# Per-layer input moved into the last MLP product, and the final norm's root without activation tables

## The chip, the cores and the metric

The kernel runs on one core of a Trainium2 chip. The metric is the device time of one execution in microseconds (us). Engines are named as in the profile: PE is TensorE's matmul and PEld its weight load, DVE is VectorE, ACT is ScalarE, POOL is GpSimd, SP is SyncE, which issues nearly all DMAs.

## The reference

A hybrid decoder layer on 512 tokens of width 1024, all in float32. Only its end is touched:

```python
u = rmsnorm(x, norm_mlp_g[i]) @ w_up[i]
x = x + jnp.square(jax.nn.relu(u)) @ w_down[i]

gate = jax.nn.sigmoid(rmsnorm(x, norm_ple_g[i]) @ w_ple_gate[i])
x = x + gate * (p[i].astype(x.dtype) @ w_ple_proj[i])
return rmsnorm(x, final_norm_g)
```

Ahead of it stand a mixer (a chunkwise mLSTM and sliding-window attention on one normalised input) and its output projection. `rmsnorm(x, g)` is `x * rsqrt(mean(x * x) + 1e-6) * g`, taken per token.

## The kernel before

**Exact products from two halves.** A float32 operand is split in two float32r tiles: the high part is a cast on ScalarE (line 134), the low part the rest, a subtraction on VectorE (line 135). A product is then three matmuls, high by high, high by low and low by high (`pairs`, line 154). Every weight is loaded whole by a DMA from SyncE into one of four buffers `wr` (`load_raw`, line 141) and split into one of four pairs `wh`, `wl` (`load_w`, line 146). Where a gain or scale is to be applied on the way, the split is lines 137 and 138.

**The order of the work.** The program is written in plain order, and Tile, the layer under it, sets the order of instructions on each engine by its own estimate of when inputs are ready, with earlier lines going first among what is ready. Each engine then runs its list in order, waiting on semaphores. SyncE's queue of DMAs is such a list too. A tile pool is a piece of SBUF; when a pool is closed, a later pool may lie on the same bytes, and a tile there waits for the readers of the tile that lay there.

**The MLP.** The 4096 hidden columns are done in four quarters (line 920). `up(q)` makes eight blocks of `uf`: matmul, relu with the token's scale, square, four sums in tile F (lines 856 to 859), split (line 861; the two halves of `uf`). `down(q)` (line 864) is a Strassen-Winograd product with seven block products instead of eight: weights are loaded into `wd` and `wr`, summed on VectorE (lines 886, 890, 904 and 910), split and multiplied, and `acc` (line 881) adds each finished PSUM pair to the residual XK (line 883). There are three such pairs of PSUM banks, X, Y and Z; line 896 adds to the running block p1. Pool `mp` holds F, rB and rt, pool `np_` holds p1, the `uf` halves and `wd`.

**The tail, lines 926 to 1003.** Both pools are closed and pool `tp` opened. The final gain is loaded to all partitions (`gfin`, line 932). For each of four token blocks of 128, p is loaded (`ptok`, line 935), transposed on TensorE (line 938) and split into `pT` (line 940). `ple(nh)` (line 942) multiplies it by one half of its projection, 24 matmuls of 512 columns, and ScalarE copies the result to `pe` (line 947). `columns_of` (line 784) makes x2, the transposed residual with its gain: for each of eight columns of 128, four transposes (line 788) into one bank of a PSUM pair and a split (lines 137 and 138). Lines 957 to 961 take the squares of each token (line 960) and the reciprocal root of their mean, `rk`: ScalarE's Sqrt (line 250) and VectorE's reciprocal (line 252).

Then the gate. Its first 512 columns are summed over four chunks of weights for all four token blocks (lines 990 to 993, 96 matmuls of 512 columns), the second 512 per token block in two halves of 256 columns from two PSUM buffers (lines 997 to 1002, 192 matmuls of 256 columns). `gate` (line 966) evicts: sigmoid with scale rk (line 968), product with `pe` (973), sum into the residual (975), sum of squares (976), and a product with `gfin` on GpSimd (977). `final(m)` (line 979) adds three sums of squares (981 and 982), takes the reciprocal root (250 and 252), scales two halves (985) and stores each (986). Line 971 is a dummy Sqrt that has the table loaded behind the last sigmoid. Sigmoid and Sqrt are in different tables of ScalarE; Square and Copy run with either.

Of the kernel before, what the change touches and what calls it, by code (L numbers as in the profile page):

```python
# [10 lines left out]
F32 = mybir.dt.float32  # L11
F32R = mybir.dt.float32r
AF = mybir.ActivationFunctionType
ALU = mybir.AluOpType
AX = mybir.AxisListType

P = 128
# [19 lines left out]
def block_kernel(  # L37
# [33 lines left out]
    def pool(stack, name, **kw):  # L71
        return stack.enter_context(tc.tile_pool(name=name, bufs=1, reuse_waits="tile", **kw))
# [13 lines left out]
    def nm(s):  # L86
        n_names[0] += 1
        return f"{s}_{n_names[0]}"


    def ps_g():
        return pp.tile([P, 512], F32, tag="g", bufs=2, name=nm("psg"))
# [38 lines left out]
    def split(dst, src, scale=None):  # L131

        if scale is None:
            A.copy(dst[0], src)  # L134
            V.tensor_sub(dst[1], src, r32(dst[0]))  # L135
        else:
            A.activation(dst[0], src, AF.Copy, scale=scale)
            V.scalar_tensor_tensor(dst[1], src, scale, r32(dst[0]), ALU.mult, ALU.subtract)
# [645 lines left out]
    def columns_of(dst, k, g):  # L784

        ps = pair()[:, 0, :]
        for m in range(NT):
            T.transpose(ps[:, m * P : (m + 1) * P], xk[m][:, k * P : (k + 1) * P], ident)
        split(dst[k], ps, g[:, k : k + 1])
# [22 lines left out]

    st_a.close()
    st_m, st_n = ExitStack(), ExitStack()
    mp = pool(st_m, "mp")
    np_ = pool(st_n, "np")
    F = lambda: mp.tile([P, 8, 256], F32, tag="F", bufs=1, name=nm("F"))

    A21, A11, A22, A12, S1, S2, S3, S4 = range(8)
# [44 lines left out]
    def down(q, uf):  # L864
# [52 lines left out]
            prod(Z, S4, form(b22[kh]), kh, False, True)  # L917
        acc(Z, 1, 1)

    for q in range(4):  # L920
        uf = []
        up(q, uf)
        down(q, uf)


    st_n.close()
    st_m.close()
    tp = pool(ctx, "tp")
    pT = [[tp.tile([P, 512], F32R, name=nm("pT")) for _ in range(2)] for _ in range(2)]
    pe = [tp.tile([P, D], F32, name=nm("pe")) for _ in range(NT)]  # L930
    gfin = tp.tile([P, D], F32, name="gfin")
    nc.sync.dma_start(out=gfin, in_=g_fin.broadcast_to([P, D]))
    for m in range(NT):
        t = tp.tile([P, PLE], F32, tag="ptok", bufs=4, name=nm("ptok"))
        nc.sync.dma_start(out=t, in_=p[m * P : (m + 1) * P, :])
        ps = ps_g()
        for k in range(2):
            T.transpose(ps[:, k * P : (k + 1) * P], t[:, k * P : (k + 1) * P], ident)
        for k in range(2):
            split([q[:, m * P : (m + 1) * P] for q in pT[k]], ps[:, k * P : (k + 1) * P])  # L940

    def ple(nh):
        w = load_w(w_pp[nh], 2 * 512, 2)
        for m in range(NT):
            ps = ps_g()
            mm_tok(ps, w, pT, m)
            A.copy(pe[m][:, nh * 512 : (nh + 1) * 512], ps)

    ple(0)
    ple(1)  # L950
    x2b, x2 = big_hl("x2")
    for k in range(8):
        columns_of(x2, k, gple)
    rk = []
    warm = cp.tile([P, 1], F32, name="warm")
    fs = cp.tile([P, NT, 4], F32, name="fs")
    for m in range(NT):
        junk = tp.tile([P, D], F32, tag="junk", bufs=1, name=nm("junk"))
        ss = small("ss", 1)
        A.activation(junk, xk[m], AF.Square, accum_out=ss)  # L960
        rk.append(rstd_of(ss, D))

    def tmp(n):
        return tp.tile([P, 512], F32, tag="tmp", bufs=8, name=nm(n))
# [1 line left out]
    def gate(m, c, n, ps):  # L966
        sg = tmp("sgp")
        A.activation(sg[:, :n], ps, AF.Sigmoid, scale=rk[m])
        if m == NT - 1 and c == D - 256:

            A.activation(warm, sg[:, :1], AF.Sqrt, bias=eps_t, scale=0.0)
        pr = tmp("prod")[:, :n]
        V.tensor_mul(pr, sg[:, :n], pe[m][:, c : c + n])
        part = xk[m][:, c : c + n]
        V.tensor_add(part, part, pr)
        A.activation(sg[:, :n], part, AF.Square, accum_out=fs[:, m, c // 256 : c // 256 + 1])
        G.tensor_tensor(part, part, gfin[:, c : c + n], ALU.mult)

    def final(m):
        ss = small("fss", 1)  # L980
        V.tensor_add(ss, fs[:, m, :1], fs[:, m, 2:3])
        V.tensor_add(ss, ss, fs[:, m, 3:])
        rs = rstd_of(ss, D)
        for c in (slice(0, 512), slice(512, D)):
            V.tensor_scalar_mul(xk[m][:, c], xk[m][:, c], rs)
            nc.sync.dma_start(out=out[m * P : (m + 1) * P, c], in_=xk[m][:, c])

    a, b = pair(), pair()
    pv = [a[:, 0, :], a[:, 1, :], b[:, 0, :], b[:, 1, :]]
    for c in range(4):  # L990
        w = load_w(w_pg[c], 2 * 512, 2)
        for m in range(NT):
            mm_tok(pv[m], w, x2[2 * c : 2 * c + 2], m, first=c == 0, last=c == 3)
    for m in range(NT):
        gate(m, 0, 512, pv[m])
    wg = [load_w(w_pg[4 + c], 2 * 512, 2) for c in range(4)]
    for m in range(NT):
        for o in (0, 256):
            ps = ps_g()[:, :256]
            for c in range(4):  # L1000
                mm_tok(ps, [q[:, :, o : o + 256] for q in wg[c]], x2[2 * c : 2 * c + 2], m, first=c == 0, last=c == 3)
            gate(m, 512 + o, 256, ps)
        final(m)

# [91 lines left out]
```

## Time and profile before

| | |
|---|---|
| three runs | 955.58, 956.19, 957.11 us, median 956.19 |
| the profiled execution | 955.62 us, span 953.9 us |
| mean granted clock of TensorE | 0.989 |
| busy: PE, DVE, ACT, POOL | 909.8, 645.6, 461.4, 33.4 us |
| chain that ended last, by engine | PE 83%, DVE 7%, ACT 5%, DMA 2%, issue 2% |

The profile is one execution. A group of instructions is named by line, engine, operation and tiles (out<-in), with its count and shape; `| busy, mean ns | idle before <-releaser` gives its busy time in us, the mean time of one in ns, and how long its engine stood idle just ahead of it and what ended that. A line is often that of a helper, so tiles tell where in the program one is: `x<-psp,gple` is x2's split, `wl<-wr` a weight's low half. In a timeline a row is start, length, engine, line, operation, tiles and count (instructions of one kind in a row are merged). A matmul's recorded length holds its drain through the array, so several in a row take less each than one alone.

### The profile page before, as it was taken

The numbers are of one execution on the slowest core, as the hardware profiler recorded it, in microseconds if no ns is written. First come the engines' busy times: TensorE is split into PE (matmuls) and PEld (weight loads), VectorE is DVE, ScalarE is ACT, GpSimd is POOL, SyncE is SP. The second block draws the span as 40 slices with busy tenths as digits, with TensorE's granted clock in tenths as the row PEclk, the third lists the DMA queues.
The fourth block names the chain that finished last, engine by engine and source line by source line (L and its number), as shares of the span: only waits on it lengthen the run. The fifth ranks groups of instructions, "written<-read, shape, count | busy, mean of one in ns | idle before, by whom it ended". The sixth has DMA issues, their size and how long they took to land.

```text
span 953.9 us, 11756 instructions
## 1 busy us (share of the span) xinstructions
PE 909.8 (95%) x4498; PEld 743.4 (78%) x4498; DVE 645.6 (68%) x992; ACT 461.4 (48%) x772; POOL 33.4 (3%) x49
## 2 busy tenths in 40 slices
PE   7959999989999999999999999999999999989995
PEld 5748999867877667788888887888788788867785
DVE  6877877454887874455654578757967885797365
ACT  7543544343685675544222545334434533435546
POOL 1000000000000000000210000000000000000032
PEclk9979999998999999999999999999999999999999
DMA  7221333631111131243352520631252063104202
GB/s 277 79 89 45 133 142 128 217 114 64 45 67 45 66 111 66 67 133 111 133 198 89 199 89 1 199 117 37 89 185 79 1 197 112 45 1 155 67 1 88
DMA packets 28602, 97.31 MB, mean 102 GB/s; under 512 B 3969, under 2 KB 4481, under 8 KB 28546
## 3 DMA queue, kind: packets, MB, share of 16 engines
q1 hardware_dynamic: 27074, 91.32, 27.9%
q0 software_dynamic: 1472, 5.24, 1.6%
q8 instruction: 35, 0.57, 0.2%
q14 instruction: 21, 0.17, 0.1%
HBM read 89.21 MB, written 7.34 MB: 101 GB/s over the span
## 4 chain that ended last, share of the span: by engine, by line
PE 83%; DVE 7%; ACT 5%; DMA 2%; issue 2%; SPq 0%; DVEq 0%; ACTq 0%
PE psg L162 49%; PE psp L162 20%; PE psa L162 6%; DVE wl L135 2%; PE pst L700 2%; ACT wh L134 2%; PE pst L627 1%; PE pst L162 1%; PE pst L690 1%; DVE uf L135 1%; PE psa L619 1%; ACT lm L601 1%; PE psa L582 1%; DMA xt<-in_x 1%; PE psa L583 1%
## 5 line engine op out<-in xcount | busy, mean ns | idle before, releaser
L135 DVE TENSOR_TENSOR wl<-wr,wh 128x1024 fp32r<-128x1024 f32 (+1 forms) x136 | 174.7, 1287 | 109.6 <-ACT wh L134 105.0
L134 ACT CAST wh<-wr 128x1024 fp32r<-128x1024 f32 (+1 forms) x136 | 142.5, 1050 | 218.5 <-PE psg L162 106.6
L162 PE MATMUL psg<-x,wh 128*128 128x512 f32 x512 | 160.1, 393 | 0.0
L162 PE MATMUL psp<-wh,uf 128*128 128x512 f32 x448 | 141.1, 394 | 2.0 <-DVE uf L135 2.0
L162 PE MATMUL psg<-h,wh 128*128 128x512 f32 x384 | 124.3, 403 | 0.6 <-DVE qs L547 0.6
L162 PEld LDWEIGHTS psg<-x,wh 128*128 128x128 f32 x512 | 96.1, 188 | 21.2
L162 PEld LDWEIGHTS psp<-wh,uf 128*128 128x128 f32 x448 | 83.8, 188 | 23.3 <-DVE uf L135 3.7
L162 PE MATMUL psg<-x,wl 128*128 128x512 f32 x256 | 100.5, 393 | 0.0
L162 PE MATMUL psp<-wl,uf 128*128 128x512 f32 x224 | 88.0, 393 | 2.0 <-DVE wl L135 2.0
L162 PEld LDWEIGHTS psg<-h,wh 128*128 128x128 f32 x384 | 71.6, 191 | 20.9 <-issue 6.6
L134 ACT CAST wh<-wd 128x1024 fp32r<-128x1024 f32 x44 | 45.9, 1051 | 70.5 <-PE psp L162 34.0
L162 PE MATMUL psg<-h,wl 128*128 128x512 f32 x192 | 76.5, 398 | 0.0
L135 DVE TENSOR_TENSOR wl<-wd,wh 128x1024 fp32r<-128x1024 f32 x44 | 53.0, 1220 | 8.8 <-ACT wh L134 8.5
L162 PEld LDWEIGHTS psg<-x,wl 128*128 128x128 f32 x256 | 48.1, 188 | 10.7
L162 PEld LDWEIGHTS psp<-wl,uf 128*128 128x128 f32 x224 | 42.1, 188 | 11.9 <-DVE wl L135 2.4
L135 DVE TENSOR_TENSOR uf<-F,uf 128x1792 fp32r<-128x1792 f32 x16 | 32.4, 2023 | 21.8 <-ACT uf L134 21.8
L162 PEld LDWEIGHTS psg<-h,wl 128*128 128x128 f32 x192 | 36.6, 191 | 9.5 <-issue 1.6
L162 PE MATMUL psg<-yb,wh 128*128 128x512 f32 x128 | 42.5, 408 | 0.0
L850 DVE SCALAR_TENSOR_TENSOR rt<-psg,rB 128x512 f32<-128x512 f32 x32 | 22.0, 688 | 27.8 <-PE psg L162 27.8
L162 PE MATMUL psg<-ya,wh 128*128 128x512 f32 x128 | 39.9, 393 | 0.0
L134 ACT CAST uf<-F 128x1792 fp32r<-128x1792 f32 x16 | 27.1, 1695 | 24.7 <-DVE F L859 24.7
L162 PE MATMUL psa<-h,wh 128*128 128x256 f32 x192 | 35.1, 284 | 0.2 <-ACT p L449 0.2
(267 smaller groups left out, 1684.3 us busy)
## 6 DMA issues: line engine op xcount, KB each, us to landing
wr<-in_w_up SPq DMA_DIRECT2D x32, 512.0 KB, 4.2
wd<-in_w_down SPq DMA_DIRECT2D x24, 512.0 KB, 4.4
gd<-gr POOLq DMA_DIRECT2D x8, 512.0 KB, 3.0
wr<-in_w_o SPq DMA_DIRECT2D x8, 512.0 KB, 3.3
wr<-in_w_qsw SPq DMA_DIRECT2D x8, 512.0 KB, 4.3
wr<-in_w_qkml SPq DMA_DIRECT2D x8, 512.0 KB, 3.2
wr<-in_w_b SPq DMA_DIRECT2D x8, 512.0 KB, 3.2
gl<-gd SPq DMA_DIRECT2D x8, 512.0 KB, 3.3
```

Source lines behind the costliest of these rows:

```text
L134: A.copy(dst[0], src)
L135: V.tensor_sub(dst[1], src, r32(dst[0]))
L162: last_mm[0] = T.matmul(ps, l, r, start=first and i == 0, stop=last and i == len(ops) - 1, skip_group_check=parts)
L582: T.matmul(o, q[:, n * P : (n + 1) * P], kk[kp][ab][:, k0 : k0 + 256], start=True, stop=False)
L583: T.matmul(o, q[:, n * P : (n + 1) * P], kl[kp][ab][:, k0 : k0 + 256], start=False, stop=True)
L601: A.activation(lm3[:, g, :], lm3[:, g, :], AF.Exp, bias=nmx[:, g : g + 1], accum_out=sm[:, g : g + 1])
L619: T.transpose(pt[:, c : c + P], lm3[ab][:, g, j * P : (j + 1) * P], ident)
L627: T.matmul(o[HALF[ab], :], vs[n + 1 - nk + j][:, c : c + 64], pTs[j][:, ab * 512 : (ab + 1) * 512], start=j == 0, stop=j == nk - 1,)
L690: T.matmul(psc[:, n0:], qk[4 + h][:, n0 : n0 + P], qk[h][:, n0:], start=True, stop=True)
L700: T.matmul(pn[:, : DV + 1], wT[s][:, t * P : (t + 1) * P], vm[s][:, h, :], start=s == 0, stop=s == t)
L850: V.scalar_tensor_tensor(a, ps, 0.0, rB, ALU.max, ALU.mult)
```

## The change

It does four things. p is loaded, transposed and split between `up(3)` and `down(3)` of the MLP, in a pool that lies where `mp` lay (`np_` and `mp` are swapped so that `mp` can be closed first). The first half of p's projection is put between x2's fourth and fifth column, the second half after the eighth, and the squares for `rk` are queued on ScalarE behind the last copy of the projections. The last norm's reciprocal root is taken on VectorE: a first guess from the bits of the sum, then three Newton steps, y <- y (3 - s y^2) / 2 without its signs and halves, which are made good by a factor in `gfin` (-sqrt(1024) / 8192, applied once on VectorE). GpSimd's product with `gfin` is gone: for the first 512 columns VectorE makes the product `z` early and ScalarE scales it, for the last 512 one VectorE instruction does both; the epsilon and two of the three sums are added ahead (`s`). The dummy Sqrt goes.

```diff
 
     st_a.close()
     st_m, st_n = ExitStack(), ExitStack()
+    np_ = pool(st_n, "np")
     mp = pool(st_m, "mp")
-    np_ = pool(st_n, "np")
     F = lambda: mp.tile([P, 8, 256], F32, tag="F", bufs=1, name=nm("F"))
 
     A21, A11, A22, A12, S1, S2, S3, S4 = range(8)
...
             prod(Z, S4, form(b22[kh]), kh, False, True)
         acc(Z, 1, 1)
 
+    def ple_rows():
+
+        ep = pool(st_n, "ep")
+        pT = [[ep.tile([P, 512], F32R, name=nm("pT")) for _ in range(2)] for _ in range(2)]
+        for m in range(NT):
+            t = ep.tile([P, PLE], F32, tag="ptok", bufs=4, name=nm("ptok"))
+            nc.sync.dma_start(out=t, in_=p[m * P : (m + 1) * P, :])
+            ps = ps_g()
+            for k in range(2):
+                T.transpose(ps[:, k * P : (k + 1) * P], t[:, k * P : (k + 1) * P], ident)
+            for k in range(2):
+                split([q[:, m * P : (m + 1) * P] for q in pT[k]], ps[:, k * P : (k + 1) * P])
+        return pT
+
     for q in range(4):
         uf = []
         up(q, uf)
+        if q == 3:
+            st_m.close()
+            pT = ple_rows()
         down(q, uf)
 
 
+    wp0 = load_w(w_pp[0], 2 * 512, 2)
     st_n.close()
-    st_m.close()
     tp = pool(ctx, "tp")
-    pT = [[tp.tile([P, 512], F32R, name=nm("pT")) for _ in range(2)] for _ in range(2)]
     pe = [tp.tile([P, D], F32, name=nm("pe")) for _ in range(NT)]
     gfin = tp.tile([P, D], F32, name="gfin")
     nc.sync.dma_start(out=gfin, in_=g_fin.broadcast_to([P, D]))
-    for m in range(NT):
-        t = tp.tile([P, PLE], F32, tag="ptok", bufs=4, name=nm("ptok"))
-        nc.sync.dma_start(out=t, in_=p[m * P : (m + 1) * P, :])
-        ps = ps_g()
-        for k in range(2):
-            T.transpose(ps[:, k * P : (k + 1) * P], t[:, k * P : (k + 1) * P], ident)
-        for k in range(2):
-            split([q[:, m * P : (m + 1) * P] for q in pT[k]], ps[:, k * P : (k + 1) * P])
-
-    def ple(nh):
-        w = load_w(w_pp[nh], 2 * 512, 2)
+
+    V.tensor_scalar_mul(gfin, gfin, -(D**0.5) / 8192)
+
+    def ple(nh, w):
         for m in range(NT):
             ps = ps_g()
             mm_tok(ps, w, pT, m)
-            A.copy(pe[m][:, nh * 512 : (nh + 1) * 512], ps)
-
-    ple(0)
-    ple(1)
+            evicted = A.copy(pe[m][:, nh * 512 : (nh + 1) * 512], ps)
+        return evicted.ins
+
     x2b, x2 = big_hl("x2")
-    for k in range(8):
+    for k in range(4):
         columns_of(x2, k, gple)
+    ple(0, wp0)
+    for k in range(4, 8):
+        columns_of(x2, k, gple)
+    evicted = ple(1, load_w(w_pp[1], 2 * 512, 2))
     rk = []
-    warm = cp.tile([P, 1], F32, name="warm")
     fs = cp.tile([P, NT, 4], F32, name="fs")
-    for m in range(NT):
-        junk = tp.tile([P, D], F32, tag="junk", bufs=1, name=nm("junk"))
-        ss = small("ss", 1)
-        A.activation(junk, xk[m], AF.Square, accum_out=ss)
-        rk.append(rstd_of(ss, D))
+    with tc.issue_after(evicted):
+        for m in range(NT):
+            junk = tp.tile([P, D], F32, tag="junk", bufs=1, name=nm("junk"))
+            ss = small("ss", 1)
+            A.activation(junk, xk[m], AF.Square, accum_out=ss)
+            rk.append(rstd_of(ss, D))
 
     def tmp(n):
         return tp.tile([P, 512], F32, tag="tmp", bufs=8, name=nm(n))
...
     def gate(m, c, n, ps):
         sg = tmp("sgp")
         A.activation(sg[:, :n], ps, AF.Sigmoid, scale=rk[m])
-        if m == NT - 1 and c == D - 256:
-
-            A.activation(warm, sg[:, :1], AF.Sqrt, bias=eps_t, scale=0.0)
         pr = tmp("prod")[:, :n]
         V.tensor_mul(pr, sg[:, :n], pe[m][:, c : c + n])
         part = xk[m][:, c : c + n]
         V.tensor_add(part, part, pr)
         A.activation(sg[:, :n], part, AF.Square, accum_out=fs[:, m, c // 256 : c // 256 + 1])
-        G.tensor_tensor(part, part, gfin[:, c : c + n], ALU.mult)
-
-    def final(m):
-        ss = small("fss", 1)
-        V.tensor_add(ss, fs[:, m, :1], fs[:, m, 2:3])
-        V.tensor_add(ss, ss, fs[:, m, 3:])
-        rs = rstd_of(ss, D)
-        for c in (slice(0, 512), slice(512, D)):
-            V.tensor_scalar_mul(xk[m][:, c], xk[m][:, c], rs)
-            nc.sync.dma_start(out=out[m * P : (m + 1) * P, c], in_=xk[m][:, c])
+
+    def one(n):
+        return tp.tile([P, 1], F32, tag=n, bufs=4, name=nm(n))
+
+    def inv_sqrt(ss):
+
+
+        bits, y, t = one("bits"), one("iy"), one("it")
+        I = mybir.dt.int32
+        V.tensor_scalar(bits.bitcast(I), ss.bitcast(I), 1, None, ALU.logical_shift_right)
+        V.tensor_scalar(y.bitcast(I), bits.bitcast(I), -1.0, float(0x5F3759DF), ALU.mult, ALU.add)
+        for three in (3.0, 12.0, 768.0):
+            V.tensor_scalar(t, y, y, ss, ALU.mult, ALU.mult)
+            V.tensor_scalar(y, t, three, y, ALU.subtract, ALU.mult)
+        return y
+
+    def final(m, s):
+
+        ss = one("fss")
+        V.tensor_add(ss, fs[:, m, 3:], s)
+        rs = inv_sqrt(ss)
+        A.activation(zs[m], zs[m], AF.Copy, scale=rs)
+        nc.sync.dma_start(out=out[m * P : (m + 1) * P, :512], in_=zs[m])
+        o = xk[m][:, 512:]
+        V.scalar_tensor_tensor(o, o, rs, gfin[:, 512:], ALU.mult, ALU.mult)
+        nc.sync.dma_start(out=out[m * P : (m + 1) * P, 512:], in_=o)
 
     a, b = pair(), pair()
     pv = [a[:, 0, :], a[:, 1, :], b[:, 0, :], b[:, 1, :]]
...
         w = load_w(w_pg[c], 2 * 512, 2)
         for m in range(NT):
             mm_tok(pv[m], w, x2[2 * c : 2 * c + 2], m, first=c == 0, last=c == 3)
+    zs = []
     for m in range(NT):
         gate(m, 0, 512, pv[m])
+        zs.append(tp.tile([P, 512], F32, name=nm("z")))
+        V.tensor_mul(zs[m], xk[m][:, :512], gfin[:, :512])
     wg = [load_w(w_pg[4 + c], 2 * 512, 2) for c in range(4)]
     for m in range(NT):
         for o in (0, 256):
...
             for c in range(4):
                 mm_tok(ps, [q[:, :, o : o + 256] for q in wg[c]], x2[2 * c : 2 * c + 2], m, first=c == 0, last=c == 3)
             gate(m, 512 + o, 256, ps)
-        final(m)
+            if o == 0:
+                s = one("fse")
+                V.tensor_scalar(s, fs[:, m, :1], fs[:, m, 2:3], D * EPS, ALU.add, ALU.add)
+        final(m, s)
```

## The prediction

> **What bounds the kernel now.** I read the page's busy times first, then busy times by stretch over the last 112 us, then TensorE's own waits there, then the timelines of the engines it waited for. A stretch's row holds its length, busy time and instructions of PE, PEld, DVE, ACT and POOL, then TensorE's granted clock, DMA share and GB/s; a wait's row holds us in total, times and the longest.
>
> ```profile
> PE 909.8 (95%) x4498; PEld 743.4 (78%) x4498; DVE 645.6 (68%) x992; ACT 461.4 (48%) x772; POOL 33.4 (3%) x49
> ```
> ```profile
> 842.00:854.00 12.00, 9.70 (x41) 7.37 (x41) 11.77 (x12) 3.15 (x3) 0.00 (x0) 1.00 0.01 2
> 854.00:875.75 21.75, 21.75 (x94) 17.69 (x95) 16.35 (x14) 8.30 (x8) 0.00 (x0) 1.00 0.28 96
> 875.75:887.87 12.12, 9.24 (x56) 6.80 (x54) 9.00 (x21) 11.40 (x29) 0.00 (x0) 1.00 0.41 132
> 887.87:898.90 11.03, 11.03 (x50) 9.01 (x48) 2.45 (x2) 5.65 (x9) 0.00 (x0) 1.00 0.28 94
> 898.90:917.82 18.92, 18.92 (x84) 15.39 (x82) 6.78 (x8) 7.23 (x8) 0.00 (x0) 1.00 0.09 29
> 917.82:934.07 16.25, 12.14 (x98) 11.52 (x96) 11.70 (x17) 9.90 (x22) 8.60 (x6) 1.00 0.02 5
> 934.07:945.74 11.67, 11.66 (x96) 11.45 (x96) 8.22 (x19) 9.50 (x18) 2.96 (x4) 1.00 0.27 100
> 945.74:953.90 8.16, 0.00 (x0) 0.00 (x0) 2.93 (x9) 3.14 (x8) 1.41 (x2) 0.72 0.29 106
> ```
> ```profile
> PE psg L162 <- ACT sgp L968: 4.1, 3, 3.1
> PE psp L162 <- DVE wl L135: 2.0, 1, 2.0
> PE psg L938 <- DMA ptok<-in_p: 1.2, 1, 1.2
> ```
>
> TensorE bounds the kernel, so a change in the tail is worth the TensorE idle time that it closes, plus what it does to the 8.16 us after the last matmul. The eight stretches are: the head of the last down product; its rest; x2's transposes; the projections (48 matmuls); the rest of the gate's first half; the first two token blocks of its second half; the last two; the tail. Two leak. In 917.82 to 934.07, 4.11 us are idle, all on ScalarE's sigmoid. In 875.75 to 887.87 idle is 2.88 us by the row, and more hides between transposes that end in a modelled time: these rows give their true cost.
>
> ```profile
> 882.37 1.04 PE L788 MATMUL psp<-ident,xk 128*128 128x128 f32 x8
> L938 PE MATMUL psg<-ident,ptok x8: 272/273/332, 881.7 to 885.0; 128*128 128x128 f32 x8
> ```
>
> Eight in a row take 1.04 us of which the last one's 0.27 is drain: a pitch of 0.11. The stretch holds 32 transposes of x2 (3.5 us), 8 of p (0.9) and 15 gate matmuls at the projections' pitch 11.03 / 48 = 0.23 (3.4): 7.8 us of 12.12, so 4.3 idle. The same row shows why: ScalarE is busy 11.40 of 12.12 us there.
>
> **The sum with no new stall.** After the change TensorE must, from 875.75 on, do 3.5 (x2's transposes) + 11.0 (projections) + 22.3 (gate, first half: 15 matmuls in 3.4 and the rest in 18.92) + 23.3 (second half, twice 11.67) = 60.1 us, ending at 935.9 instead of 945.74: 9.8 us sooner. Counted the other way: 4.3 + 0.9 + 4.1 + 0.5 (12.14 against 11.67) = 9.8. From this I take off what the change adds.
>
> **p's transposes in the last down product.** They need p, which can be requested only once the pool under it is free; the last reader of F there is VectorE's uf split.
>
> ```profile
> 840.25 2.02 DVE L135 TENSOR_TENSOR uf<-F,uf 128x1792 fp32r<-128x1792 f32 x1
> 851.57 1.23 DVE L883 TENSOR_TENSOR xk<-psp,xk 128x1024 f32<-128x1024 f32 x1 [0.23 <-PE psp L162]
> 852.71 3.48 DVE L135 TENSOR_TENSOR wl<-wd,wh 128x1024 fp32r<-128x1024 f32 x3
> 853.98 0.50 PE L162 MATMUL psp<-wl,uf 128*128 128x512 f32 x1 [1.98 <-DVE wl L135]
> L135 DVE TENSOR_TENSOR pT<-psg,pT 128x128 fp32r<-128x128 f32 x8 | 2.0, 286 | 1.3 <-ACT pT L134 1.2
> ptok<-in_p SPq DMA_DIRECT2D x4, 128.0 KB, 5.2
> gfin<-in_g_fin SPq DMA_DIRECT2D x1, 512.0 KB, 5.4
> ```
> ```profile
> 876.35 1.85 SPq L935 DMA_DIRECT2D ptok<-in_p  x4
> ```
>
> The last column of the two DMA rows is the median us from issue to landing; four issues take SyncE 1.85 us. Requested at 842.3, p's pieces land from about 847.5 (5.2) to 848.9 (1.4 later), before 851.57. VectorE is the late engine just there (11.77 of 12.00 us busy), with 0.23 us of slack before the add at 851.57 that stands ahead of the wl split for which TensorE waits 1.98 us. Eight subtractions of p add 2.0 us of VectorE: 1.7 us of delay. On TensorE eight transposes (0.9) and a wait for p (1.2 in the trace) ahead of that add would make it 2.1. If they fall behind 852.71, only their 0.9, or as little as 0.2 inside the 1.98 idle. I take 1.7, nearest the row of p's landing, between 0.2 and 3. ScalarE's eight casts fit: it is busy 3.15 of 12 us. After 854 TensorE has no slack, so all of this goes to the end.
>
> **x2's stage.** What kept ScalarE busy:
>
> ```profile
> L137 ACT ACTIVATE x<-psp,gple 128x512 fp32r<-128x512 f32 x8 | 5.0, 691 | 0.0
> L960 ACT ACTIVATE junk<-xk 128x1024 f32<-128x1024 f32 x4 | 4.3, 1065 | 1.7 <-PE psp L162 1.7
> L947 ACT COPY pe<-psg 128x512 f32<-128x512 f32 x7 | 4.1, 588 | 4.8 <-PE psg L162 4.8
> L138 DVE SCALAR_TENSOR_TENSOR x<-psp,gple,x 128x512 fp32r<-128x512 f32 x8 | 5.6, 745 | 1.6 <-ACT x L137 1.6
> ```
>
> The squares (4.3 us and their small reads and roots) go behind the last projection's copy, and p's casts leave. x2's splits (5.0 on ScalarE, 5.6 on VectorE) and eight copies (8 x 0.588 = 4.7) lie beside 14.5 us of TensorE work. The order covers them: four columns' splits (2.8 us) under the first projections (5.5), four under the second. The squares then run under the gate's first half (22.3), which waits for them only at its sigmoids. The third PSUM pair is free only after the last add of the MLP, as now. The added wait is gfin's scaling on VectorE, at most 1 us, not before 875.95 + 5.4 = 881.3; queued behind it are x2's subtractions, and behind these TensorE's transposes, with 5.5 us of projections as cover; without that cover it costs up to 5.4 + 0.9 - 3.5 (x2's own transposes) = 2.8. I allow 0.6 us in this stage (0.2 to 2). The weight of the first projection loads ahead as before, and the swap of the two pools far ahead only moves addresses: both at nothing, since a weight's load is covered by the products before it; uncovered it is one load.
>
> **The gate.** Why the sigmoids were late:
>
> ```profile
> 930.63 1.28 ACT L250 ACT_TABLE_LOAD   x1
> 932.24 1.28 ACT L968 ACT_TABLE_LOAD   x1
> 934.07 0.38 PE L162 MATMUL psg<-wh,x 128*128 128x256 f32 x1 [3.12 <-ACT sgp L968]
> L975 DVE TENSOR_TENSOR xk<-xk,prod 128x512 f32<-128x512 f32 x4 | 4.7, 1206 | 0.0
> 917.15 1.29 DVE L975 TENSOR_TENSOR xk<-xk,prod 128x512 f32<-128x512 f32 x2
> 920.34 5.72 POOL L977 TENSOR_TENSOR xk<-xk,gfin 128x512 f32<-128x512 f32 x3 [428.73 <-ACT sgp L976]
> ```
>
> Of 3.12 us, 2.56 are two table loads for the root of the first block; they go with the root. The other 1.0 us follows slow VectorE adds: the four take 4.7, of which two 1.29 before GpSimd starts at 920.34, so 1.7 each beside it. Without GpSimd VectorE gets four products more: 12 x 0.65 = 7.8 us plus a weight split of 1.2 (852.71: three in 3.48), against 3 x 6 matmuls x 0.23 = 4.1 us from the first block's end to the last's and two PSUM buffers of 11.67 / 4 = 2.9 us each. That is 9.0 of 9.9, close: I allow 0.9 us (0 to 2). In the second half a block costs VectorE four ops of 0.42, ten small ones of 0.2 and one of 0.7, about 4.4 us of TensorE's 5.8; ScalarE, at 0.40 for a square and 0.69 for a scaling, less. No stall.
>
> **The tail after the last matmul.**
>
> ```profile
> 946.26 1.28 ACT L971 ACT_TABLE_LOAD   x1
> 946.73 0.42 DVE L975 TENSOR_TENSOR xk<-xk,prod 128x256 f32<-128x256 f32 x1
> 947.75 0.40 ACT L976 ACTIVATE sgp<-xk 128x256 f32<-128x256 f32 x1
> 949.10 0.29 ACT L250 ACTIVATE sd<-fss,eps_t 128x1 f32<-128x1 f32 x1 [0.45 <-DVE fss L982]
> 949.42 0.16 DVE L252 RECIPROCAL rs<-sd 128x1 f32<-128x1 f32 x1 [0.36 <-ACT sd L250]
> 949.62 0.88 DVE L985 TENSOR_SCALAR xk<-xk,rs 128x512 f32<-128x512 f32 x2
> 370.13 0.16 DVE L706 SCALAR_TENSOR_TENSOR den<-hd 128x4 f32<-128x4 f32 x1
> 370.33 0.17 DVE L707 TENSOR_TENSOR den<-den,gc 128x4 f32<-128x4 f32 x1
> ```
>
> Now the add ends at 947.15, the warming load holds the square to 947.75, and 1/root is there at 949.58. After: square at 947.17 in these times, its sum half a microsecond later, one add, then eight dependent tiny operations at 0.20 each (370.13 to 370.33): 1.6 us, ready at 949.5. Then ScalarE scales one half (0.69) while VectorE does the other (0.745), against 0.88 for the pair; the second store leaves about 0.35 after the first, as now. Tail: 0, within 0.4 either way.
>
> A rule speaks against this. The Trainium skill (ScalarE: Activation LUTs, What it computes) says to get a reciprocal root from VectorE's reciprocal and ScalarE's Sqrt. By it the tail would keep the 0.48 us from 949.10 to 949.58 and lose the 0.6 of the held square: 0.5 shorter than the 1.6 of tiny operations, 949.1 instead of the forecast below; the trace agrees on that link, and shows what roots on ScalarE cost at the first block, 3.12. The same page (What ACT_TABLE_LOAD costs) puts a switch at about 2.66 us, 1.38 of it drain; the trace has 1.28 with the next instruction 0.02 later (930.63 + 1.28 = 931.91, and the root is over by 932.24).
>
> **The sum.** 9.8 - 1.7 - 0.6 - 0.9 = 6.6 us. The profiled execution took 955.62 (span 953.9 and 1.7 around it), so 949.0; the median of the runs is 956.19, 0.6 above it, and 6.6 below that is 949.6, my forecast.
>
> **Rivals.** (A) Everything is covered: p falls into the 1.98 us gap (0.2), the hand-overs cost 0.4; 9.2 saved, 947.0. For: the gap is long enough; against: p lands before it. (B) The hand-overs go wrong while the moves succeed: gfin's wait costs 2 and the gate's first block 2; 9.8 - 1.7 - 4 = 4.1, 952.1. For: VectorE's 9.0 of 9.9. (C) Slower: TensorE's order puts p's transposes ahead of the last down product's first matmuls. It stands from 842.3 until the fourth piece lands (6.6 us), then 0.9 of transposes; VectorE's adds, which need those matmuls, follow with p's 1.7: 9.2 us. With 1.5 of hand-overs 10.7 against 9.8: 0.9 lost, 957.1. It decides from 8.3 us on. Against: in the trace TensorE's order has transposes of x2 ahead of p's, so it goes by arrival, missing by 1.2 us. (D) The overlap doesn't come: projections stay behind all eight columns, and p's 1.7 with new hand-overs eat the rest: 955.5.
>
> **How the numbers follow.** Forecast 0.60, A 0.13, B 0.19, C 0.04, D 0.04. The range reaches A's 947.0 and B's 952.1, with the tail's 0.4 on either side: 946.6 to 952.5. What is left out is C, D and terms that all fall at their bounds. About 0.2% (1.9 us) is what a measurement of this kernel can tell from no change: faster 0.92, same 0.04, slower 0.04.
>
> **What would show it.** Right: no table load after the first sigmoid; no TensorE wait over 1 us on sigmoids; 875.75's stage with under 1 us of idle; the wait at 853.98 longer by about 1.7; the last matmul 8.1 us ahead of the end. Wrong: a wait on ptok of several us, or TensorE waiting for VectorE between the projections.

## The result, and the profile after

The kernel went from a median of 956.65 us (955.58 to 958.07, four runs) to 950.37 us (949.43 to 952.49, four runs): 6.3 us less, a ratio of 0.9917 with a 95% interval of 0.9893 to 0.9942. The profiled execution took 950.01 us, its span 948.3 us, at a mean granted clock of 0.987.

The busy line of the page after: GpSimd's work in the tail is gone, ScalarE has 8 instructions fewer, VectorE 29 more, and TensorE does what it did.

```profile
PE 909.0 (96%) x4498; PEld 744.1 (78%) x4498; DVE 646.7 (68%) x1021; ACT 454.3 (48%) x764; POOL 20.4 (2%) x37
```

Busy time by stretch, after: head of the last down product, its rest, x2's transposes with the first projection, the rest of the projections and most of the gate's first half, then the gate's second half in two, and the tail. Columns as in the prediction.

```profile
843.47:857.07 13.60, 10.65 (x49) 8.18 (x49) 13.16 (x20) 4.72 (x11) 0.00 (x0) 1.00 0.14 40
857.07:878.85 21.78, 21.78 (x94) 17.70 (x95) 16.37 (x14) 8.31 (x8) 0.00 (x0) 1.00 0.27 97
878.85:893.89 15.04, 15.00 (x81) 12.18 (x80) 9.64 (x12) 10.74 (x17) 0.00 (x0) 1.00 0.40 139
893.89:915.99 22.10, 22.10 (x98) 18.02 (x96) 7.25 (x12) 12.25 (x20) 0.00 (x0) 1.00 0.08 25
915.99:927.66 11.67, 11.67 (x98) 11.50 (x97) 10.79 (x28) 7.72 (x20) 0.00 (x0) 1.00 0.01 1
927.66:939.11 11.45, 11.45 (x97) 11.24 (x96) 8.94 (x31) 5.51 (x15) 0.00 (x0) 1.00 0.25 92
939.11:948.30 9.19, 0.00 (x0) 0.00 (x0) 3.75 (x13) 1.74 (x6) 0.00 (x0) 0.77 0.31 114
```

From 857.07 to 939.11 the second and third numbers are the same but for 0.04 us: TensorE has no idle time in x2's stage (2.88 us before) and none in the gate's second half (4.11 us before). TensorE's waits from 841 us to the end of the span confirm it; two are left, both in the last down product:

```profile
PE psp L162 <- DVE wl L135: 2.9, 1, 2.9
PE psp L162 <- DVE uf L135: 0.5, 1, 0.5
```

TensorE's timeline after. p's transposes start at 845.93 and wait for nothing; x2's transposes come in groups of four or eight between the first projection's products, not all ahead of them:

```profile
845.93 0.38 PE L929 MATMUL psg<-ident,ptok 128*128 128x128 f32 x2
...
857.07 0.50 PE L162 MATMUL psp<-wl,uf 128*128 128x512 f32 x1 [2.89 <-DVE wl L135]
...
878.85 1.03 PE L788 MATMUL psp<-ident,xk 128*128 128x128 f32 x8
...
880.33 0.66 PE L788 MATMUL psp<-ident,xk 128*128 128x128 f32 x4
```

VectorE's timeline after, with the subtractions for p (the first and the last of eight) between the split of uf and the add to the residual:

```profile
841.45 2.02 DVE L135 TENSOR_TENSOR uf<-F,uf 128x1792 fp32r<-128x1792 f32 x1
...
846.79 0.28 DVE L135 TENSOR_TENSOR pT<-psg,pT 128x128 fp32r<-128x128 f32 x1
...
852.00 0.49 DVE L135 TENSOR_TENSOR pT<-psg,pT 128x128 fp32r<-128x128 f32 x2 [0.20 <-ACT pT L134]
...
854.67 1.22 DVE L883 TENSOR_TENSOR xk<-psp,xk 128x1024 f32<-128x1024 f32 x1
855.80 3.48 DVE L135 TENSOR_TENSOR wl<-wd,wh 128x1024 fp32r<-128x1024 f32 x3
```

From the end of the uf split to the weight split for which TensorE waits it was 10.44 us before (842.27 to 852.71) and is 12.33 us now: 1.89 us later.

A ledger of the closing stretch, from the end of that uf split to the end of the span (the code ahead of it is unchanged), made from the timelines:

| us | before | after | gain |
|---|---|---|---|
| uf split to the end of the last down product | 33.64 | 35.54 | -1.90 |
| x2, projections, gate's first half | 41.91 | 36.98 | 4.93 |
| gate's second half | 27.91 | 23.12 | 4.79 |
| tail after the last matmul | 8.17 | 9.19 | -1.02 |
| closing stretch | 111.63 | 104.83 | 6.80 |

In the profiled execution of after the stretch began 1.2 us later (843.47 against 842.27), in unchanged code where TensorE ran at half clock for longer between 205 and 230 us (mean granted clock there 0.80 against 0.86); so the span shows 5.6 of the 6.8.

### The profile page after: what moved, and what is told of

It reads as the page before. It is cut to its first block, busy times and chain, and to the rows that moved or that the text cites. A ratio compares the mean times of both kernels' runs of the same rounds, so it can differ in the third digit from the quotient of the medians.

```text
span 948.3 us, 11750 instructions
## 1 busy us (share of the span) xinstructions
PE 909.0 (96%) x4498; PEld 744.1 (78%) x4498; DVE 646.7 (68%) x1021; ACT 454.3 (48%) x764; POOL 20.4 (2%) x37
## 4 chain that ended last, share of the span: by engine, by line
PE 85%; DVE 8%; ACT 4%; issue 1%; DMA 1%; SPq 0%; ACTq 0%; DVEq 0%
PE psg L162 49%; PE psp L162 20%; PE psa L162 6%; PE pst L700 2%; DVE wl L135 2%; PE pst L627 1%; ACT wh L134 1%; PE pst L162 1%; PE pst L690 1%; DVE uf L135 1%; PE psa L619 1%; PE psp L788 1%; PE psa L582 1%; PE psa L583 1%; DMA xt<-in_x 1%
```

## The experiments

Each kernel is the changed one with one edit; where an edit changes what is computed, it says so. Where no median is given, a time and a row of the ledger are from one execution. The ledger leaves out what happens upstream, so the experiments are read from it. A stage that an edit does not touch repeats there within 0.1 us (x2 to the gate's first half 36.96 to 37.02, second half 23.12 or 23.13, tail 9.17 to 9.25), apart from the last down product:

| kernel | closing | last down product | x2 to gate's first half | second half | tail |
|---|---|---|---|---|---|
| e1_p_late | 108.33 | 33.64 | 42.35 | 23.12 | 9.22 |
| e2_proj_behind | 107.39 | 37.10 | 37.93 | 23.12 | 9.24 |
| e3_squares_free | 106.47 | 37.17 | 37.00 | 23.12 | 9.18 |
| e4_root_on_act | 108.28 | 37.15 | 37.02 | 23.12 | 10.99 |
| e5_gpsimd_back | 110.5 | 37.13 | 36.96 | 25.41 | 11.0 |
| e6_two_steps | 105.97 | 37.11 | 36.99 | 23.12 | 8.75 |
| e7_store_on_act | 106.61 | 37.12 | 37.01 | 23.12 | 9.36 |
| e8_p_in_second_half | 103.55 | 34.28 | 36.97 | 23.13 | 9.17 |
| e9_changed_again | 106.45 | 37.15 | 37.01 | 23.12 | 9.17 |
| e10_sums_later | 104.93 | 35.58 | 36.98 | 23.12 | 9.25 |
| e11_later_two | 103.21 | 34.26 | 36.99 | 23.12 | 8.84 |
| e12_all_three | 104.81 | 35.85 | 37.01 | 23.12 | 8.83 |

The 37.1 where the changed kernel's profile has 35.54 comes up under e9.

**e1: p back behind the MLP.**

```diff
-            pT = ple_rows()        # between up(3) and down(3), pool ep on st_n
+    pT = ple_rows()                # after gfin's load and scaling, pool tp
```

> p is loaded, transposed and split after the MLP, in the pool where it was before; everything else as changed. Measure: the closing stretch, from the end of the last uf split on VectorE to the end of the span (before 111.6 us, changed kernel 104.8). Theory (the sum of the prediction): p's 1.9 us in the down product come back, so its rest shortens, but p cannot be asked for before the down product ends, the projections start only after it lands, and TensorE stands in x2's stage again: 3 to 4 us lost there, closing stretch 106 to 107. Rival (Tile fills the wait with the gate's first matmuls, so the early transposes only cost): 103, faster than the changed kernel by the 1.9.

952.30 us. The down product has its 33.64 us back, and x2's stage loses 5.4, more than the 3 to 4 that my theory gave: the closing stretch is 108.33, not 106 to 107. Early p is worth 3.5 net against the changed kernel's first profile (104.83), and 1.9 against its second (e9, 106.45), which lost 1.6 us to the clock. TensorE's waits and p's DMA in this kernel:

```profile
PE psp L162 <- DVE wl L135: 2.0, 1, 2.0
PE psp L788 <- DVE x L138: 1.1, 1, 1.1
PE psg L945 <- DMA ptok<-in_p: 1.1, 1, 1.1
PE psp L162 <- ACT pT L134: 0.5, 1, 0.5
...
ptok<-in_p SPq DMA_DIRECT2D x4, 128.0 KB, 5.6
```

The wl wait is at before's 2.0 again, and p's own chain (ptok, pT) with x2's splits behind it is what stood in x2's stage. With p late that stage takes 42.35 us against 41.91 before: the new places of the projections and squares bring nothing without early p. The rival's 103 us for the stretch is wrong.

**e2: both projections behind all eight columns.**

```diff
-    for k in range(4):
-        columns_of(x2, k, gple)
-    ple(0, wp0)
-    for k in range(4, 8):
+    for k in range(8):
         columns_of(x2, k, gple)
+    ple(0, wp0)
```

> Both halves of the projection stand behind x2's eight columns instead of one half between the fourth and fifth; p stays early. Theory (rival D of the prediction, that the place between the columns is what covers x2's splits): VectorE's eight splits of 0.745 us set the pace of the transposes, 6 us against TensorE's 3.5, so the closing stretch grows by 2 to 2.5 us, to 107. Rival (p being ready early is all that matters, since Tile orders TensorE by readiness and takes projection matmuls whenever a transpose waits): within 0.4 us of 104.8.

951.77 us, and 37.93 instead of 36.98 in that stage: the place is worth 1.0 us, less than my theory and more than the rival. One row of TensorE's timeline holds it:

```profile
886.78 0.66 PE L788 MATMUL psp<-ident,xk 128*128 128x128 f32 x4 [0.89 <-DVE x L138]
```

Even written behind all columns, projection products slip in between the columns, since pT and their weight are ready long before; the written place only decides the last bit. (The closing stretch of 107.39 is near the 107 of my theory only by the 1.6 us of the clock in the down product.)

**e3: the squares no longer held behind the projections.**

```diff
-    with tc.issue_after(evicted):
+    if True:
```

> The squares for rk are no longer queued behind the last projection copy on ScalarE. Theory: ScalarE was busy 11.4 of 12.1 us in x2's stage, squares and roots took 5.6 of it, so with them back among the splits x2's stage grows by 1 to 2 us: closing stretch 106 to 107. Rival (with p's casts gone and the projections as cover ScalarE has room for them): within 0.4 us of 104.8.

950.64 us. The first square moves from 894.58 to 877.71, right into x2's stage, and that stage takes 37.00 instead of 36.98: nothing. With p's casts gone, ScalarE has the room: it is busy 10.74 of 15.04 us there in the changed kernel, and 13.94 with the squares back (e3, 879.34 to 894.38), while TensorE stays busy all 15.04. This part of the change bought nothing.

**e4: the roots back on ScalarE, GpSimd still out of it.** The dummy Sqrt behind the last sigmoid is back too, and gfin is left unscaled to fit.

```diff
-        rs = inv_sqrt(ss)
+        rs = rstd_of(ss, D)
```

> The last norm's reciprocal root is again ScalarE's Sqrt and VectorE's reciprocal, with the dummy Sqrt behind the last sigmoid; GpSimd stays out and p stays early. Theory: the two table loads at each of the first three blocks come back, and the sigmoid that waits behind the first pair stalls TensorE about 3 us as before; the tail after the last matmul gets 0.4 to 0.6 us shorter, since the eight tiny operations took 2.0 us where root and reciprocal take 0.5 and the load holds the square 0.6. Closing stretch 107 to 107.5. Rival (the stall came from GpSimd holding up VectorE, not from the table loads): no TensorE wait on a sigmoid over 1 us, closing stretch 104.3.

956.22 us, but not for the reason in my theory. The second half of the gate stays at 23.12 us, and TensorE has no wait in it. ScalarE's timeline:

```profile
929.35 0.47 ACT L980 ACTIVATE sgp<-psg,rs 128x256 f32<-128x256 f32 x1 [0.18 <-PE psg L162]
929.84 1.28 ACT L250 ACT_TABLE_LOAD   x1
...
932.46 1.28 ACT L980 ACT_TABLE_LOAD   x1
...
944.33 1.28 ACT L980 ACT_TABLE_LOAD   x1
945.62 0.47 ACT L980 ACTIVATE sgp<-psg,rs 128x256 f32<-128x256 f32 x1
```

The same pair of loads as before stands around the first block's root, but the sigmoid that frees a PSUM buffer ran ahead of it, and the next one (933.76) is in time. Loads alone did not stall TensorE here. Where they do cost is the end: the last sigmoid starts at 945.62, 2.1 us after the last matmul's end at 943.5, behind the loads for the third block's root; the tail takes 10.99 us, 1.8 more.

**e5: GpSimd's product back, roots left on VectorE.** The last scaling then leaves gfin out, as before the change.

```diff
+        G.tensor_tensor(part, part, gfin[:, c : c + n], ALU.mult)
```

> The product with the last gain is on GpSimd again, after each sum into the residual; the Newton steps stay, p stays early. Putting the root back on ScalarE had given no TensorE wait in the gate (second half 23.1 us as in the changed kernel, before 27.9), so the table loads alone are not the cause of the 3.1 us. Theory: the stalls need GpSimd, which holds VectorE's adds back by 1 us each, so that squares and what stands behind them on ScalarE come late; without table loads this costs 1 us (the 0.7 and 0.3 that the trace of before has at the first block), second half 24.1, and the tail grows by up to 1 since GpSimd's product is in it. Rival: GpSimd alone makes all of the 4.8 us, second half 27 or more. Second rival: neither alone costs anything, second half 23.1, and the stall needed both together.

958.23 us beside 957.99 before. The gate's second half takes 2.3 us more, between the 1.0 of my theory and the 4.8 of the first rival, with TensorE waiting as follows, and the groups of VectorE's adds and of GpSimd's products show why:

```profile
PE psg L162 <- ACT sgp L980: 1.4, 3, 0.7
```
```profile
L984 DVE TENSOR_TENSOR xk<-xk,prod 128x512 f32<-128x512 f32 x4 | 4.7, 1205 | 0.0
...
L986 POOL TENSOR_TENSOR xk<-xk,gfin 128x512 f32<-128x512 f32 x4 | 7.0, 1766 | 428.8 <-ACT sgp L985 428.8
```

The same group in the changed kernel, without GpSimd:

```profile
L984 DVE TENSOR_TENSOR xk<-xk,prod 128x512 f32<-128x512 f32 x4 | 2.7, 684 | 0.0
```

So GpSimd alone costs 2.3 in the gate, the loads alone 0, and in the kernel before, where both stood, they cost 4.8: not a sum of two prices. In the kernel before, the root of the first block stands in ScalarE's list ahead of the sigmoid that was due (loads from 930.63, sigmoid at 933.54); in e4 that sigmoid stands ahead of the root. The lists are fixed when the program is built, so a late add cannot have changed them during the run. Why Tile ordered them so, no run isolates; that the order, and not GpSimd's hold, makes the rest of the 4.8 is an open rival.

The tail grows by 1.8 us as well, where I had expected up to 1: the last sigmoid starts at 947.29, 2.1 us after the last matmul's end (945.20), behind the third block's scaling, for which ScalarE had waited 2.18 us.

**e6: two Newton steps instead of three,** so the root is coarser; by how much no run here records.

```diff
-        for three in (3.0, 12.0, 768.0):
+        for three in (3.0, 12.0):
```

> Two Newton steps instead of three for the last norm's root (the scale in the gain is then sqrt(1024)/16). Theory: the tail after the last matmul is one chain, of which a step is two dependent operations, 0.27 and 0.21 us long at a pitch of 0.56 us for both, so the tail goes from 9.2 to 8.6 us. Rival: the stores set the end (two issues of 0.35 us and a landing of 2.1 to 2.3), and the tail stays within 0.2.

953.10 us; tail 8.75, 0.44 less. A step costs somewhat less than the pitch of its two instructions, 0.56 (below).

**e7: the last block's first store issued by ScalarE.**

```diff
+        store = nc.scalar if m == NT - 1 else nc.sync
```

> The store of the last block's first half is issued by ScalarE instead of SyncE; nothing else changes. Theory: both halves are ready within 0.05 us of one another, SyncE issues them one after the other and the second starts 0.42 later, so with two issuers the end comes 0.3 to 0.4 us sooner: tail 8.8. Rival: the DMA engines, not the issue, set the second store's end: within 0.15.

953.79 us; tail 9.36, so nothing is gained. This store lands 2.8 us after issue against 2.1 for the three from SyncE: what the earlier issue saved was lost before the landing. Whether ScalarE's queue or the two stores moving at once make it slower is not separated.

**e8: p in the second half of the last down product,** behind the fifth of its seven block products, ahead of the product with A22.

```diff
         acc(Z, 0, 1)
+        if q == 3:
+            ple_rows()
```

> p is loaded, transposed and split in the second half of the last down product, ahead of its A22 block product, instead of before it. Theory: at the head VectorE is the late engine and p's eight subtractions and the two ScalarE waits between them make TensorE wait 2.9 us instead of 2.0 for a weight's low half, 1.9 us with the transposes; in the second half VectorE and ScalarE have gaps of 1.5 us, so only the transposes' 0.9 stays: from the last uf split to the end of the last down product 34.5 us against 35.5, the wait at the weight's low half back at 2.0. The granted clock, which after the wait of 2.9 us fell to 0.79 to 0.97 for some 8 us in three of four executions and cost 1.6 us more there, stays at 1.00 after a wait of 2.0. Rival: the wait comes back at another weight split, and 35.5 stays.

951.05 us beside 957.99 before; the down product takes 34.28 us, 1.3 less than the changed kernel's. TensorE's wait for the weight's low half is before's again, with p's subtractions behind it in VectorE's timeline:

```profile
PE psp L162 <- DVE wl L135: 1.9, 1, 1.9
```
```profile
860.79 0.48 DVE L135 TENSOR_TENSOR pT<-psg,pT 128x128 fp32r<-128x128 f32 x2
```

That leaves 0.64 of the 1.90 us, a bit less than the eight transposes' 0.9, which TensorE must do somewhere. Tile put four of the transposes ahead of the wait all the same (849.05 and 855.14); it is VectorE's part that now comes behind it. That the clock stayed at 1.00 after a wait of 1.9 us was not certain: e12 shows the other case.

**e9: the changed kernel again,** timed in five rounds beside e11 and e12.

> The changed kernel as it is, timed beside the two better ones. Theory: its wait of 2.9 us in the last down product is followed in most executions by a drop of the granted clock that costs 1.6 us, so its times lie at two levels 1.6 us apart, the lower one the rarer; ratio to the kernel before 0.993 to 0.995. Rival (the drops are a matter of the chip or the hour): no drop in its profile, 35.5 us from the last uf split to the end of the last down product.

Median 951.33 us (950.21 to 953.89, six runs), ratio 0.9926 (0.9904 to 0.9948). The kernel before ranged from 955.59 to 960.49 us beside it (eleven runs, median 959.94, granted clock 0.982 to 0.989), so here the changed kernels are compared with one another. The two levels that I expected do not show: this profile, with the drop, is the fastest of the six, as what happens upstream differs by as much. In this profile the down product takes 37.15 us with the same instructions and the same wait of 2.9 us. Busy time by stretch; the number after POOL's is the granted clock:

```profile
852.00:856.00 4.00, 1.10 (x5) 0.50 (x4) 4.00 (x5) 0.00 (x0) 0.00 (x0) 1.00 0.00 0
856.00:860.00 4.00, 4.00 (x12) 3.16 (x11) 3.00 (x3) 0.89 (x1) 0.00 (x0) 0.59 0.00 0
860.00:864.00 4.00, 4.00 (x18) 3.21 (x17) 2.38 (x3) 2.16 (x3) 0.00 (x0) 0.99 0.00 0
```

The last of these stretches in the changed kernel's first profile:

```profile
860.00:864.00 4.00, 4.00 (x19) 3.26 (x18) 2.81 (x4) 3.05 (x3) 0.00 (x0) 1.00 0.00 0
```

After the wait TensorE gets a clock of 0.59 over four microseconds: 12 matmuls in 4.00 us busy, against 18 in the next stretch and 19 in the first profile. At half clock that is 4.00 x 0.41 / 0.5 = 3.3 us, and 0.1 in the next stretch, half of which is lost: 1.7 us, against a measured 37.15 less 35.54, 1.6. The changed kernel's first profile caught the lucky case.

**e10: the three sums of p1 after the next products,** to bring the waited-for weight split forward.

```diff
-        if q == 3:
-            for toks, n in ((1, 1), (0, 0), (0, 1)):
-                acc(p1, toks, n)
         acc(Y, 1, 1)
...
             V.tensor_sub(b21[kh], b21[kh], b11[kh])
+        if q == 3:
+            for toks, n in ((1, 1), (0, 0), (0, 1)):
+                acc(p1, toks, n)
```

> In the last down product the three adds of the running block into the residual stand behind the two b21 weights instead of ahead of them; p stays at the head. Theory: these 3 x 1.13 us of VectorE are what the weight's low half waits behind; taken away, the wait of 2.9 us shrinks to under 1 us, the granted clock stays at 1.00, and the last down product ends 33 us after the last uf split (changed kernel 35.5 without the drop, 37.1 with it). It shows the drop hanging on the wait and not on p's place. Rival (the drop comes from p's transposes in between): clock under 1 at 860 to 868 all the same.

949.96 us, 35.58 in the down product. TensorE's wait, and VectorE's timeline:

```profile
PE psp L162 <- DVE wl L135: 3.2, 1, 3.2
```
```profile
852.30 2.35 DVE L883 TENSOR_TENSOR xk<-p,xk 128x1024 f32<-128x1024 f32 x2
...
855.70 3.49 DVE L135 TENSOR_TENSOR wl<-wd,wh 128x1024 fp32r<-128x1024 f32 x3
```

The experiment failed to do what it was for: Tile put the adds ahead of the split all the same. Whether the wait is behind these adds stays untested. What it does show is a wait of 3.2 us with no drop of the clock.

**e11: e8 and e6 together; e12: these two and e10's edit.**

> p in the second half of the last down product and two Newton steps: the two that helped. Theory: 34.3 us to the end of the last down product with the clock at 1.00, 37.0, 23.1 and a tail of 8.75: closing stretch 103.1 us against 111.6 before, ratio 0.991. Rival: the two do not add, over 103.6.

> As the one with p in the second half and two steps, and the three adds behind the b21 weights too. Theory: the wait of 1.9 us at the weight's low half goes as well, the last down product ends 32.5 us after the last uf split; closing stretch 101.3, ratio 0.989. Rival (VectorE is late again further on, where p and the adds now stand together): 34.3 stays.

e11: closing stretch 103.21 us, median 948.90 us (948.07 to 951.87, six runs), ratio 0.9904 (0.9880 to 0.9928): 2.4 us below the changed kernel's 951.33 in the same batch, with five of its six runs below that one's lowest (950.21). Its median is the lowest here, with the coarser root. e12: 949.59 us (947.86 to 951.36, six runs). Its wait is still 1.88 us, so the moved adds gain nothing, and its profile has the drop after a short wait, from TensorE's timeline and from the busy time by stretch:

```profile
856.48 0.76 PE L162 MATMUL psp<-wl,uf 128*128 128x512 f32 x1 [1.88 <-DVE wl L135]
```
```profile
856.00:860.00 4.00, 3.52 (x8) 2.79 (x9) 4.00 (x6) 0.08 (x1) 0.00 (x0) 0.57 0.00 0
```

## Why the prediction was right, point by point

The forecast was 949.6 us, 6.6 below before's median; measured are 950.37 and 6.3. The frame held: TensorE bounds the kernel, the change is worth the idle time it closes, and from x2's first transpose to the last matmul TensorE took 60.3 us (878.85 to 939.11) against the stall-free 60.1. The terms, however, met the total partly by luck: of what I took off, the hand-overs were 1.3 us too much, p 0.2 and the tail 1.0 too little, and the profile compared has none of the clock's drop (last point below).

- **The 9.8 us of idle time: right.** No table load follows the first sigmoid, no wait on sigmoids is left, and x2's stage is idle for 0.04 us.
- **"0.6 us in this stage" and "0.9 us" for the gate: too much.** Both together came to 0.2 us. gfin's scaling was feared as a new wait; it runs at 884.83, behind 1.44 us in which VectorE only waits, and nobody behind it is late. Rival A, that everything is covered, had this right, but not p. Rival B's 4 us of hand-overs are not there; D falls with the interleaved transposes, and C with p's transposes, for which TensorE never stood.
- **p's 1.7 us: right in size (1.90) and mechanism, with a wrong step under it.** The VectorE delay of 1.89 is the eight subtractions. But I took p's landing from its row, 5.2 us, and that was the price of p behind gfin's 512 KB. Asked for alone:

```profile
ptok<-in_p SPq DMA_DIRECT2D x4, 128.0 KB, 2.3
gfin<-in_g_fin SPq DMA_DIRECT2D x1, 512.0 KB, 5.8
```

  With p back behind gfin (e1) it is 5.6 again. A latency from a queue with something large ahead is not the latency of the transfer. Landing from 845.8 (843.5 + 2.3) rather than from 847.5 should have changed no time, since VectorE was the late engine. The wait on wl grew by 0.91 (1.98 to 2.89), not by 1.7: the other microsecond is the eight transposes, which fill the rest of the time that TensorE has while VectorE is late.
- **"Of 3.12 us, 2.56 are two table loads for the root": failed as an attribution.** With the loads back and GpSimd gone (e4) the gate loses nothing; with GpSimd back and the loads gone (e5) it loses 2.3. Where the loads held TensorE up, a root stood in front of a due sigmoid; what put it there stays open (e5). The wait named the last to come, which alone costs the gate nothing. The sum survived because the change removed both.
- **"Tail: 0": failed by 1.0 us;** the last matmul lies 9.2 us ahead of the end, not 8.1. The timeline of the tail after, all engines, and SyncE's issues:

```profile
940.63 0.42 ACT L985 ACTIVATE sgp<-xk 128x256 f32<-128x256 f32 x1 [1.01 <-DVE xk L984]
941.17 0.16 DVE L1005 TENSOR_TENSOR fss<-fs,fse 128x1 f32<-128x1 f32 x1 [0.63 <-ACT sgp L985]
941.37 0.15 DVE L995 TENSOR_SCALAR bits<-fss 128x1 int32<-128x1 int32 x1
...
941.74 0.27 DVE L998 TENSOR_SCALAR it<-iy,fss 128x1 f32<-128x1 f32 x1
942.05 0.21 DVE L999 TENSOR_SCALAR iy<-it,iy 128x1 f32<-128x1 f32 x1
942.30 0.27 DVE L998 TENSOR_SCALAR it<-iy,fss 128x1 f32<-128x1 f32 x1
...
943.42 0.75 DVE L1010 SCALAR_TENSOR_TENSOR xk<-xk,iy,gfin 128x512 f32<-128x512 f32 x1
943.42 0.72 ACT L1007 ACTIVATE z<-z,iy 128x512 f32<-128x512 f32 x1 [2.28 <-DVE iy L999]
944.17 0.33 SPq L1008 DMA_DIRECT2D out<-z  x1
944.59 0.38 SPq L1011 DMA_DIRECT2D out<-xk  x1
```

  The eight tiny operations take 2.05 us (941.37 to 943.42), not 1.6: those that read scalars from tiles of one column take 0.27 (two such scalars) and 0.21 (one) instead of 0.15 or 0.16, and a step is 0.56 apart (941.74 to 942.30). e6, one step less, gives 0.44 back. From the last matmul to 1/root it is 4.31 us against 3.84 before (945.74 to 949.58): 0.47. The first store leaves 0.75 after the root instead of 0.55 (950.13): 0.2. The last 0.35, from the second store's issue to the end (3.71 against 3.36), stays open; moving one store to another queue (e7) did not get it back.
- **The rule on the root.** The Trainium skill (ScalarE: Activation LUTs, What it computes) would have the root from ScalarE's Sqrt and VectorE's reciprocal, and by it the tail was to be 0.5 us shorter. The trace agrees on the link: in e4 the last 1/root is there 0.68 us after the sum (948.89 to 949.57), against 2.25 with Newton (941.17 to 943.42). But the tables it needs put 2.1 us between the last matmul and its sigmoid, and the tail came out 1.8 longer. The rule is about the operation; here the switches of tables around it counted for more.
- **What was not in the sum: the clock.** p's place costs 1.9 or 3.5 us, by whether TensorE's clock halves after the wait it lengthens. In e9's profile it cost 3.5. The prediction had no term for it; before's own wait of 1.98 us could have been followed by it too, and in its profile was not.

## What to carry to other kernels

Before you charge a stall to what its last wait names, ask what made that come late, and take the named one away alone or leave it in alone: here the table loads were named, and by themselves they cost the gate nothing. Take a transfer's latency from a row where nothing large is queued ahead of it, and a chain of tiny operations from rows with the same kind of operands. If work moved under a busy TensorE loads an engine that TensorE waits for, put it behind that wait, not ahead of it: p a few products later costs 0.6 us instead of 1.9, and 2.2 (e12's 35.85 less 33.64) instead of 3.5 where the clock drops.

## What the runs showed of the hardware that I had not expected

TensorE's granted clock can fall to half for 3.4 us after a wait of only two to three microseconds. Of the nine profiles here with the wait for wl at 2.9 us or more it followed in seven (e2 to e7 and e9) and not in two (the changed kernel's first, and e10 at 3.2); of the five with 1.9 to 2.0 us it followed in one (e12). Before's own wait of 3.12 us at 934.07 was followed by a clock of 1.00. It costs 1.6 us each time.

The length of the wait does not decide it, but the traces show what goes with it. In each profile the granted clock changes only at points that lie multiples of 3.41 us apart, and these points lie elsewhere in each execution. So a wait falls into one such window or is split between two. The table gives, for each profile, the window with the least TensorE work around the wait for wl, and the clock granted in the window behind it.

| profile | wait for wl, us | window, us | TensorE busy in it, of 3.41 us | clock in the next window |
|---|---|---|---|---|
| e8 | 1.87 | 853.60 to 857.01 | 2.05 | 1.00 |
| e1 | 1.98 | 850.18 to 853.59 | 1.82 | 1.00 |
| after | 2.89 | 855.33 to 858.75 | 1.68 | 1.00 |
| before | 1.98 | 850.39 to 853.81 | 1.61 | 1.00 |
| e11 | 1.87 | 852.18 to 855.59 | 1.61 | 1.00 |
| e10 | 3.18 | 855.16 to 858.57 | 1.60 | 1.00 |
| e12 | 1.88 | 853.14 to 856.55 | 1.53 | 0.50 |
| e6 | 2.90 | 857.00 to 860.41 | 1.50 | 0.50 |
| e7 | 2.90 | 857.06 to 860.48 | 1.39 | 0.50 |
| e2 | 2.89 | 854.24 to 857.66 | 1.36 | 0.50 |
| e5 | 2.90 | 857.24 to 860.65 | 1.36 | 0.50 |
| e4 | 2.90 | 857.63 to 861.04 | 1.22 | 0.50 |
| e3 | 2.90 | 853.63 to 857.04 | 1.10 | 0.50 |
| e9 | 2.90 | 853.27 to 856.68 | 1.03 | 0.50 |

All eight drops stand below 1.6 us of work in a window, all six others at 1.6 or above. Before's wait of 3.12 us fits: it was split, with 1.66 us of work in its emptier window (932.31 to 935.72). Elsewhere in these programs the border is less sharp: apart from each program's first window, 1.53 us or less was always followed by half clock, 1.69 or more never, and between them both occur. So the changed kernel's first profile was lucky in where its windows lay, and e8's shorter wait makes a drop less likely but does not rule it out. No run shifts a wait against the windows on purpose.

The Trainium skill (TensorE: Matmul & The Clock Gate, Part 1: The HAM clock gate) says that the clock falls to half after an idle window of about 3.4 us, that these windows run freely and do not start with the kernel, and that how a run meets them varies. The trace agrees on half clock, on the window's length and on its free place; it does not agree that a window has to be idle throughout, since 1.88 us without work in one window were enough in e12.
